# Output products of a stage's second token half, ranked behind the transpositions of the first half's next norm

## The chip, the cores and the metric

The kernel runs on one core of a Trainium2 chip. The metric is the device time of one execution in microseconds (us), lower is better; the time of a kernel is the median over its runs.

## The reference

A chain of ten residual stages over S = 256 tokens of width D = 1024, in fp32: FFN, differential attention, FFN, FFN, spatial gating (SGU), FFN, HGRN2, convolutional FFN, NSA (sparse attention), convolutional FFN. Each stage normalizes the stream, modulates it, runs its mixer, and adds the gated output back:

```
mod = silu(c) @ ada_w[i] + ada_b[i]
sh1, sc1, g1, sh2, sc2, g2, sh3, sc3, g3 = jnp.split(mod, N_MOD, axis=-1)
h = modulate(rms_norm(x, ln_ffn1[i]), sh1, sc1)
x = x + 0.5 * g1[:, None, :] * swiglu(h, ffn1_wg[i], ffn1_wu[i], ffn1_wd[i])
h = modulate(rms_norm(x, ln_mix[i]), sh2, sc2)
...
x = x + g2[:, None, :] * mix
h = modulate(rms_norm(x, ln_ffn2[i]), sh3, sc3)
x = x + 0.5 * g3[:, None, :] * swiglu(h, ffn2_wg[i], ffn2_wu[i], ffn2_wd[i])
x = rms_norm(x, ln_out[i])
```

Here `modulate(h, shift, scale)` is `h * (1 + scale) + shift` and `swiglu` is `(silu(h @ wg) * (h @ wu)) @ wd` with D_FF = 2816. Every stage ends in such an output matrix (`wd`, `w_o`, `w_out`), and the next stage can begin only with a norm over whole rows of the x that this matrix completes.

## The kernel before

**Tokens and products.** The 256 tokens are two halves of 128, h = 0 and h = 1 (first and second half). Each fp32 factor is split in a high and a low part (`whi`, `wlo` of a weight, `hhi`, `hlo` of the normed input, `ahi`, `alo` of the inner activation), and each product is three matmuls: high by high, high by low, low by high. The high part of a weight is made by ScalarE (ACT), the low part, `wlo<-raw,whi`, by VectorE (DVE). Weights come in 1 MB loads (`raw`).

**The end of a stage.** The output matrix accumulates in four PSUM tiles `pd`, two column blocks for each half. `down` adds inner blocks for both halves as they come, and keeps back the last few (`SKEW`: 4, 5 or 6). For the kept blocks it first finishes the first half (`down_rest(0)`); the second half's products of these blocks are `rest`: two column blocks of SKEW x 3 matmuls with 512 columns, 24, 30 or 36 in all. The closure `end` in `run` then writes, for each half: `residual` (`gy<-pd,gb`, the gate, and `x<-x,gy`, the sum, on DVE, twice 512 columns), and `norm`. Between the first half's residual and its norm it calls `rest()`.

**The norm.** `x_rstd` squares x on ACT with a row sum (`xs<-x`, then a read of the accumulator), `rstd` adds the two sums on DVE (`ss<-ss`) and takes the power -1/2 on GpSimd (POOL `ss<-ss,mhalf`). `norm` scales x into `xs` (first 512 columns on DVE, second on ACT), transposes it by eight matmuls of 128 columns (`xT<-ident,xs`), modulates each transposed block on ACT (`h<-xT,mcol`, eight of them), casts pairs on DVE (`hhi<-h`) and subtracts (`hlo<-h,hhi`, two of them). After stages 2 and 5 `norm_twice` does two norms in one, with the product `xrow<-x,raw` before. The next stage's first products take `hhi` of the first half. They are called `pqk` and `pv` (attention), `pgv` (FFN, SGU), `pig` (HGRN2) and `px` (conv FFN and NSA); a boundary is written 0→1 for the end of stage 0 and the start of stage 1.

**Who sets the order.** Nothing is issued as written. The class `Plan` records all operations with a rank, by which a list scheduler then puts each engine's program in one fixed order (`order`): an engine that comes free in the planner's own clock takes the operation of lowest rank whose inputs are there and whose tiles have slots.

```
op.prio = len(self.ops) + self.shift
```

`shift` is 0 but where a few places raise it (`NSA`, `FIRST`), so the rank is otherwise the number of the operation as written. Slots of tiles are handed out by rank too. All operations are issued by one helper, so the profile shows line 514 for each; tile names tell them apart. The last stage (i = 9) ends in the output and has no norm behind it in this form; stage 8 calls `end` with the halves swapped and a `rest` of its own, 48 products that also wait for two reloaded weights.

Of the kernel before, what the change touches and what calls it, by code (L numbers as in the profile page):

```python
# [525 lines left out]
ADA_PE = (9,)  # L526
RATE = 0.92
FIRST = 20

SKEW = {0: 4, 1: 4, 2: 6, 3: 4, 4: 4, 5: 6, 6: 4, 7: 5, 9: 4}  # L530
NSA = (250, 150, 20)
# [2 lines left out]
class Model:  # L534
# [458 lines left out]
    def first(self, wg, wu):  # L993
# [80 lines left out]
        def products(k):  # L1074
            nc.shift = FIRST
            for h in range(2):
                hs = slice(128 * h, 128 * h + 128)
                for c in range(3):
                    o = acc[h][c]
                    hi, lo = parts[k][c]  # L1080
                    nc.tensor.matmul(o, hhi[:, k, hs], hi, start=k == 0, stop=False)
                    nc.tensor.matmul(o, hhi[:, k, hs], lo, start=False, stop=False)
                    nc.tensor.matmul(o, hlo[:, k, hs], hi, start=False, stop=k == 7)
            nc.shift = 0
# [765 lines left out]
    def run(self, out):  # L1850
        nc, a = self.nc, self.a
        self.x = [self.C.tile([128, D], F32, name=f"x{h}") for h in range(2)]
        self.setup()
        self.warm(4)
        self.load_c()
        self.warm(10)
        blocks = {0: 29, 1: 16, 2: 33, 3: 33, 4: 12, 5: 33, 6: 20, 7: 33, 8: 15, 9: 33}
        prep = {4: self.sgu_prep, 6: self.hgrn_prep, 8: self.nsa_prep}
        self.acc, self.mcols, self.bcol, self.grow, self.col = {}, [], {}, {}, {}
        self.halves = (0, 1)  # L1860
        acts = self.first(a["ffn1_wg"][0], a["ffn1_wu"][0])
        for i in range(10):
            self.bg = []
            self.now = i
            if i in self.grow:
                self.bg.append(lambda i=i: self.gate_load(i))
            for item in ADA[i]:
                self.bg += self.mod_steps(item, item[1] in ADA_PE)
                if item == ("g", i):
                    self.bg.append(lambda i=i: self.gate_load(i))  # L1870
            if i == 0:
                self.bg[5:5] = [lambda: self.load_columns(("ln_mix", "ln_ffn2"), "cols1", [a["ada_b"][1]], 3)]
                self.bg[12:12] = [self.load_columns2]
                self.bg[15:15] = [self.attn_bias]
                self.bg[18:18] = [self.attn_lambda]
            if i == 2:
                self.bg[4:4] = [
                    lambda: self.load_columns(("norm_mix_2", "norm_ffn_2"), "cols3", [a["ada_b_2"][0]], 6),
                    lambda: self.load_columns(("sgu_ln_g", "hg_lb_2"), "cols4", [a["ada_b_2"][1]], 8)]
            self.bg_rate = len(self.bg) / (blocks[i] * RATE)  # L1880
            self.bg_due = 0.0
            if i in prep:
                prep[i]()
            row = None
            if i in (2, 5):
                row = self.load_row(a["ln_out"][i // 3])
            if i == 9:
                row = self.load_row(a["final_norm_2"])

            def end(halves=(0, 1), rest=self.down_rest, i=i, row=row):  # L1890
                self.flush()
                gb_now = self.gb
                if i < 9:
                    self.norm_begin()
                self.halves = halves
                for h in halves:
                    self.residual(h, gb_now)
                    if h == halves[0]:
                        rest()
                    if i == 9:  # L1900
                        y = self.xs()
                        r = self.x_rstd(h, y)
                        for c in range(2):
                            cs = slice(512 * c, 512 * c + 512)
                            nc.vector.scalar_tensor_tensor(y[:, cs], self.x[h][:, cs], r, row[:, cs], op0=OP.mult,
                                                           op1=OP.mult)
                            nc.sync.dma_start(out[0, 128 * h:128 * h + 128, cs], y[:, cs])
                    elif i in (2, 5):
                        self.norm_twice(h, row)
                    else:  # L1910
                        self.norm(h)

            if i in (0, 2, 3, 5):
                l, j = divmod(i, 3)
                nm = "ffn1" if j == 0 else "ffn2"
                self.ffn(a[nm + "_wg"][l], a[nm + "_wu"][l], a[nm + "_wd"][l], end, acts if i == 0 else ())
            elif i == 1:
                self.attention(end)
            elif i == 4:
                self.sgu(end)  # L1920
            elif i == 6:
                self.hgrn(end)
            elif i == 8:
                self.nsa(end)
            else:
                l = (i - 7) // 2
                self.conv_ffn(l, a["ffn_w_up_2"][l], a["ffn_w_down_2"][l], end)
# [24 lines left out]
```

## Time and profile before

| | |
|---|---|
| time, median of 3 runs | 1709.83 us (1709.03 to 1711.03) |
| time of the profiled execution | 1712.62 us |
| its span in the trace | 1710.8 us |
| TensorE (PE) busy | 1678.8 us, 98% |
| weight loads of TensorE (PEld) | 1508.2 us, 88% |
| VectorE (DVE) | 1309.8 us, 77% |
| ScalarE (ACT) | 947.0 us, 55% |
| GpSimd (POOL) | 65.1 us, 4% |
| mean granted clock of TensorE | 0.992 of 2.4 GHz |

The span is what the trace shows of one execution; 1.8 us of that execution's time lie outside it. A row of a timeline gives the start, the duration, the engine, the operation (output <- inputs, sizes), how many in a row, and in brackets how long the engine was idle before it and for what. Matmuls overlap one another in the pipe: one of 512 columns takes 0.39 us, but the next one starts 0.23 us after it.

### The profile page before, as it was taken

The numbers are of one execution on the slowest core, as the hardware profiler recorded it, in microseconds if no ns is written. First come the engines' busy times: TensorE is split into PE (matmuls) and PEld (weight loads), VectorE is DVE, ScalarE is ACT, GpSimd is POOL, SyncE is SP. The second block draws the span as 40 slices with busy tenths as digits, with TensorE's granted clock in tenths as the row PEclk, the third lists the DMA queues.
The fourth block names the chain that finished last, engine by engine and source line by source line (L and its number), as shares of the span: only waits on it lengthen the run. The fifth ranks groups of instructions, "written<-read, shape, count | busy, mean of one in ns | idle before, by whom it ended". The sixth has DMA issues, their size and how long they took to land.

```text
span 1710.8 us, 30956 instructions
## 1 busy us (share of the span) xinstructions
PE 1678.8 (98%) x12662; PEld 1508.2 (88%) x12662; DVE 1309.8 (77%) x1951; ACT 947.0 (55%) x1581; POOL 65.1 (4%) x60
## 2 busy tenths in 40 slices
PE   8999999999999999999999999999999999999998
PEld 6899789899988999788999889989998886689986
DVE  4887689987777877677877787889897547888754
ACT  4544467564445544374644368877554556766542
POOL 0000012100001000001000000000000000000000
PEclk9999999999999999999999999999999998999999
DMA  9998865678896998676688975357888565257662
GB/s 319 332 323 297 274 229 201 209 245 264 295 327 203 340 305 315 220 243 223 225 281 307 317 240 174 110 181 247 275 287 314 176 202 218 87 168 227 221 210 74
DMA packets 258191, 415.25 MB, mean 243 GB/s; under 512 B 12938, under 2 KB 204277, under 8 KB 257025
## 3 DMA queue, kind: packets, MB, share of 16 engines
q1 hardware_dynamic: 258049, 413.27, 71.7%
q8 instruction: 99, 1.62, 0.4%
q14 instruction: 43, 0.35, 0.1%
HBM read 412.14 MB, written 1.10 MB: 242 GB/s over the span
## 4 chain that ended last, share of the span: by engine, by line
PE 67%; DVE 4%; DMA 4%; ACT 3%; issue 1%; POOL 0%; DVEq 0%; POOLq 0%; ACTq 0%; SPq 0%
PE pd L514 18%; PE pv L514 16%; PE pg L514 8%; PE pa L514 7%; PE pq L514 3%; PE pig L514 3%; DMA raw<-in_ffn_wd 2%; DVE wlo L514 2%; PE pf L514 1%; DMA raw<-in_ffn_wu 1%; PE pgv L514 1%; ACT whi L514 1%; DMA raw<-in_ada_w 1%; PE px L514 1%; PE no L514 1%
## 5 line engine op out<-in xcount | busy, mean ns | idle before, releaser
L514 ACT ACTIVATE whi<-raw 128x1024 fp32r<-128x1024 f32 x508 | 530.8, 1057 | 525.8 <-PE pd L514 136.9
L514 DVE TENSOR_TENSOR wlo<-raw,whi 128x1024 fp32r<-128x1024 f32 x508 | 611.8, 1220 | 216.6 <-ACT whi L514 212.2
L514 DVE SCALAR_TENSOR_TENSOR acc<-raw,csil,acc 128x1024 f32<-128x1024 f32 x192 | 246.0, 1281 | 16.1 <-DMA raw<-in_ada_w 13.5
L514 PE MATMUL pv<-hhi,wlo 128*128 128x256 f32 x896 | 252.6, 282 | 0.0
L514 PE MATMUL pv<-hlo,whi 128*128 128x256 f32 x896 | 252.2, 281 | 0.0
L514 PE MATMUL pv<-hhi,whi 128*128 128x256 f32 x896 | 252.1, 281 | 0.0
L514 PE MATMUL pd<-whi,ahi 128*128 128x512 f32 x604 | 239.5, 398 | 0.7 <-ACT whi L514 0.7
L514 PE MATMUL pd<-wlo,ahi 128*128 128x512 f32 x604 | 238.2, 394 | 0.1
L514 PE MATMUL pd<-whi,alo 128*128 128x512 f32 x604 | 237.9, 395 | 0.0
L514 PE MATMUL pg<-hhi,whi 128*128 128x256 f32 x608 | 172.2, 283 | 0.0
L514 PE MATMUL pg<-hhi,wlo 128*128 128x256 f32 x608 | 171.8, 283 | 0.0
L514 PEld LDWEIGHTS pv<-hhi,whi 128*128 128x128 f32 x896 | 170.4, 190 | 1.2 <-issue 1.2
L514 PE MATMUL pg<-hlo,whi 128*128 128x256 f32 x608 | 171.5, 282 | 0.0
L514 PEld LDWEIGHTS pv<-hhi,wlo 128*128 128x128 f32 x896 | 170.4, 190 | 0.0
L514 PEld LDWEIGHTS pv<-hlo,whi 128*128 128x128 f32 x896 | 170.3, 190 | 0.0
L514 PEld LDWEIGHTS pd<-whi,ahi 128*128 128x128 f32 x604 | 113.4, 188 | 32.9 <-issue 6.1
L514 PEld LDWEIGHTS pd<-whi,alo 128*128 128x128 f32 x604 | 113.4, 188 | 25.9 <-issue 0.2
L514 PEld LDWEIGHTS pd<-wlo,ahi 128*128 128x128 f32 x604 | 113.4, 188 | 25.4 <-DVE wlo L514 0.5
L514 PEld LDWEIGHTS pg<-hhi,whi 128*128 128x128 f32 x608 | 115.6, 190 | 2.6 <-issue 1.7
L514 PEld LDWEIGHTS pg<-hhi,wlo 128*128 128x128 f32 x608 | 115.6, 190 | 0.1
L514 PEld LDWEIGHTS pg<-hlo,whi 128*128 128x128 f32 x608 | 115.6, 190 | 0.0
L514 PE MATMUL pa<-hhi,whi 128*128 128x256 f32 x352 | 99.3, 282 | 0.0
(361 smaller groups left out, 3126.1 us busy)
## 6 DMA issues: line engine op xcount, KB each, us to landing
raw<-in_ada_w SPq DMA_DIRECT2D x118, 1024.0 KB
raw<-in_ffn_wd SPq DMA_DIRECT2D x44, 1024.0 KB
raw<-in_ffn_w_up SPq DMA_DIRECT2D x44, 1024.0 KB
raw<-in_ffn_wg SPq DMA_DIRECT2D x41, 1024.0 KB
raw<-in_ffn_wu SPq DMA_DIRECT2D x41, 1024.0 KB
raw<-in_ffn_w_down SPq DMA_DIRECT2D x22, 1024.0 KB
raw<-in_hg_w_in SPq DMA_DIRECT2D x16, 1024.0 KB
raw<-in_attn_w_qkv SPq DMA_DIRECT2D x12, 1024.0 KB
```

What stands on the lines that cost most here:

```text
L514: f(*[real(v) for v in args], **{k: real(v) for k, v in kw.items()})
```

## The change

One constant and two assignments: while `rest()` is recorded, 80 is added to the rank of each of its operations. The norm of one half is about 28 operations, so the second half's kept products stand behind the first half's norm in rank, about beside the second half's norm, which needs them, and the first operations of the next stage. Nothing is added to or taken from the computation.

```diff
 ADA_PE = (9,)
 RATE = 0.92
 FIRST = 20
+REST = 80
 
 SKEW = {0: 4, 1: 4, 2: 6, 3: 4, 4: 4, 5: 6, 6: 4, 7: 5, 9: 4}
 NSA = (250, 150, 20)
@@ -1896,7 +1897,10 @@
                 for h in halves:
                     self.residual(h, gb_now)
                     if h == halves[0]:
+
+                        nc.shift = REST
                         rest()
+                        nc.shift = 0
                     if i == 9:
```

The planner turns these ranks into orders. TensorE at 0→1: the last rows of `rest` (`pd`) and the first half's transpositions.

```order
 L514 MATMUL pd<-whi,alo 128x512
 L514 MATMUL pd<-whi,ahi 128x512
-L514 MATMUL pd<-wlo,ahi 128x512
-L514 MATMUL pd<-whi,alo 128x512
-L514 MATMUL pd<-whi,ahi 128x512
-L514 MATMUL pd<-wlo,ahi 128x512
-L514 MATMUL pd<-whi,alo 128x512
 L514 MATMUL xT<-ident,xs 128x128 x8
+L514 MATMUL pd<-wlo,ahi 128x512
+L514 MATMUL pd<-whi,alo 128x512
+L514 MATMUL pd<-whi,ahi 128x512
+L514 MATMUL pd<-wlo,ahi 128x512
```

The eight transpositions moved ahead of the last five products of `rest`; a fifth follows the four that are shown. At the other boundaries the tail behind the transpositions is 8 products (2→3), 10 (3→4), 5 (4→5), 9 (5→6), 12 (7→8) and about 33 (8→9). At 6→7 and in stage 9's end nothing moved.

TensorE at 1→2, before: the last product of the first half (`pd_3434` is its second column block), then `rest` (`pd_3450` and `pd_3556`, 24 products), then the transpositions.

```order
L514 MATMUL pd_3434<-wlo_3665,ahi_3713 128x512
L514 MATMUL pd_3434<-whi_3629,alo_3724 128x512
L514 MATMUL pd_3450<-whi_3529,ahi_3458 128x512
L514 MATMUL pd_3450<-wlo_3616,ahi_3458 128x512
...
L514 MATMUL pd_3556<-wlo_3665,ahi_3713 128x512
L514 MATMUL pd_3556<-whi_3629,alo_3724 128x512
L514 MATMUL xT_3790<-ident_84,xs_3748 128x128 x2
```

After, at the same place; the second half's blocks are `pd_3525` (four rows here) and `pd_3532` (seven rows).

```order
L514 MATMUL pd_3434<-wlo_3672,ahi_3728 128x512
L514 MATMUL pd_3434<-whi_3619,alo_3740 128x512
L514 MATMUL pd_3525<-whi_3573,alo_3740 128x512
L514 MATMUL pd_3525<-whi_3619,ahi_3728 128x512
...
L514 MATMUL pd_3532<-wlo_3672,ahi_3728 128x512
L514 MATMUL pd_3532<-whi_3619,alo_3740 128x512
L514 MATMUL xT_3801<-ident_84,xs_3777 128x128 x2
```

Between the first half's last product and its transpositions there were 24 products of `rest`, and now there are 11; the other 13 run earlier, before or among the first half's. After these transpositions eight products of the next stage are issued before the second half's transpositions; before the change there were 33.

VectorE at 2→3, before: the second half's residual (`gy`, `x1`, `xrow`) among the first half's casts (`hhi`, `hlo`).

```order
L514 TENSOR_TENSOR wlo_5797<-raw_5626,whi_5781 128x1024
L514 TENSOR_TENSOR gy_5815<-pd_5350,gb_4536 128x512
L514 CAST hhi_5818<-h32_5811 128x2x128
L514 TENSOR_TENSOR x1_103<-x1_103,gy_5815 128x512
L514 CAST hhi_5818<-h32_5811 128x2x128
L514 TENSOR_TENSOR hlo_5836<-h32_5811,hhi_5818 128x4x128
L514 CAST hhi_5818<-h32_5822 128x2x128 x2
L514 TENSOR_TENSOR hlo_5836<-h32_5822,hhi_5818 128x4x128
L514 TENSOR_TENSOR xrow_5861<-x1_103,raw_3537 128x512
L514 TENSOR_SCALAR ss2_5793<-ss2_5793 128x1
L514 TENSOR_TENSOR wlo_5871<-raw_5626,whi_5854 128x1024
```

After, at the same place:

```order
L514 CAST hhi_5807<-h32_5797 128x2x128
L514 TENSOR_TENSOR wlo_5811<-raw_5626,whi_5781 128x1024
L514 CAST hhi_5807<-h32_5797 128x2x128
L514 CAST hhi_5807<-h32_5814 128x2x128
L514 TENSOR_TENSOR hlo_5831<-h32_5797,hhi_5807 128x4x128
L514 CAST hhi_5807<-h32_5814 128x2x128
L514 TENSOR_TENSOR hlo_5831<-h32_5814,hhi_5807 128x4x128
L514 TENSOR_TENSOR gy_5855<-pd_5350,gb_4536 128x512
L514 TENSOR_TENSOR lbt_5863<-cols4_4408 128x8
L514 TENSOR_TENSOR x1_103<-x1_103,gy_5855 128x512
L514 TENSOR_TENSOR xrow_5874<-x1_103,raw_3543 128x512
L514 TENSOR_TENSOR wlo_5877<-raw_5626,whi_5852 128x1024
```

The second half's last `gy` and `x1` moved behind all of the first half's casts, `xrow` behind them, and the low part of the next weight (`wlo_5871`, now `wlo_5877`) behind `xrow`. On ACT the squares of the second half, one or two of which stood ahead of the first half's eight `h`, now all stand behind them. The order at 5→6 moved in the same way; at 0→1 and 4→5 `gy` and `x1` moved behind two or three of the casts. The queue of loads (SP) did not change but for one exchange of two rows, and POOL's changed in one row.

## Rows read from the trace of the kernel before

**Rows 1.** The page, busy times: engine, us, share of the span, instructions.
```profile
PE 1678.8 (98%) x12662; PEld 1508.2 (88%) x12662; DVE 1309.8 (77%) x1951; ACT 947.0 (55%) x1581; POOL 65.1 (4%) x60
```

**Rows 2.** Waits of TensorE: tile that waited, releaser, us in total, times, longest.
```profile
PE xT L514 <- DVE xs L514: 3.7, 4, 1.3
PE pgv L514 <- DVE hhi L514: 2.5, 4, 0.9
...
PE px L514 <- DVE hhi L514: 1.8, 2, 1.0
...
PE pqk L514 <- DVE hhi L514: 1.3, 1, 1.3
...
PE pig L514 <- DVE hhi L514: 1.0, 2, 0.6
```

**Rows 3.** Timeline of TensorE, then of ACT, at 0→1.
```profile
226.89 1.04 PE L514 MATMUL xT<-ident,xs 128*128 128x128 f32 x8
229.25 0.39 PE L514 MATMUL pqk<-whi,hhi 128*128 128x256 f32 x1 [1.32 <-DVE hhi L514]
...
227.87 2.88 ACT L514 ACTIVATE h<-xT,mcol 128x128 f32<-128x128 f32 x8
```

**Rows 4.** Timeline of TensorE at 1→2.
```profile
338.89 0.39 PE L514 MATMUL pd<-whi,alo 128*128 128x512 f32 x1
...
344.67 1.03 PE L514 MATMUL xT<-ident,xs 128*128 128x128 f32 x8
346.27 0.38 PE L514 MATMUL pgv<-whi,hhi 128*128 128x256 f32 x1 [0.57 <-DVE hhi L514]
...
351.36 1.09 PE L514 MATMUL xT<-ident,xs 128*128 128x128 f32 x8 [0.87 <-DVE xs L514]
```

**Rows 5.** Timelines of ACT and of POOL at 1→2.
```profile
343.77 0.70 ACT L514 ACTIVATE xs<-x,ss 128x512 f32<-128x512 f32 x1
...
342.54 0.56 POOL L514 TENSOR_TENSOR ss<-ss,mhalf 128x1 f32<-128x1 f32 x1 [8.75 <-DVE ss L514]
349.32 1.47 POOL L514 TENSOR_TENSOR ss<-ss,mhalf 128x1 f32<-128x1 f32 x1 [6.22 <-DVE ss L514]
```

**Rows 6.** Timeline of TensorE at 2→3.
```profile
538.68 0.39 PE L514 MATMUL pd<-whi,alo 128*128 128x512 f32 x1
538.91 1.03 PE L514 MATMUL xT<-ident,xs 128*128 128x128 f32 x8
540.54 0.38 PE L514 MATMUL pgv<-whi,hhi 128*128 128x256 f32 x1 [0.59 <-DVE hhi L514]
...
545.23 0.39 PE L514 MATMUL pgv<-wlo,hhi 128*128 128x256 f32 x1 [0.55 <-DVE wlo L514]
...
547.00 0.61 PE L514 MATMUL xT<-ident,xs 128*128 128x128 f32 x4
...
548.61 0.38 PE L514 MATMUL pgv<-whi,hhi 128*128 128x256 f32 x1 [0.45 <-DVE hhi L514]
```

**Rows 7.** Timelines of DVE and of ACT at 2→3.
```profile
542.62 0.69 DVE L514 TENSOR_TENSOR hlo<-h,hhi 128x512 fp32r<-128x512 f32 x1
543.23 0.68 DVE L514 TENSOR_TENSOR xrow<-x,raw 128x512 f32<-128x512 f32 x1
...
537.04 1.07 ACT L514 ACTIVATE whi<-raw 128x1024 fp32r<-128x1024 f32 x1 [0.87 <-PE pd L514]
```

**Rows 8.** Timelines of TensorE and of DVE at 4→5.
```profile
816.27 0.38 PE L514 MATMUL pgv<-whi,hhi 128*128 128x256 f32 x1 [0.92 <-DVE hhi L514]
821.69 1.09 PE L514 MATMUL xT<-ident,xs 128*128 128x128 f32 x8 [0.66 <-ACT xs L514]
...
819.26 1.21 DVE L514 TENSOR_TENSOR wlo<-raw,whi 128x1024 fp32r<-128x1024 f32 x1
```

**Rows 9.** Two windows in stage 8: busy us (instructions) by engine, granted clock, DMA.
```profile
1428.00:1432.00 4.00, 2.42 (x28) 1.93 (x24) 2.00 (x5) 2.71 (x6) 0.00 (x0) 1.00 0.86 343
1432.00:1448.00 16.00, 15.95 (x67) 7.71 (x67) 10.60 (x38) 9.52 (x27) 0.00 (x0) 0.57 0.67 244
```

## The prediction

> **What bounds the kernel now.** I read the busy times first: TensorE works for 98% of the span [rows 1], so time can only be won where it stands still, or lost where it comes to stand still. Next I read what it waits for [rows 2]. The waits that this change can touch are of two kinds. One is the wait of the next stage's first product for the cast `hhi`: 2.5 us for `pgv`, 1.8 for `px`, 1.3 for `pqk`, 5.6 in all. The other is the wait of the transpositions for `xs`, 3.7 us in four places.
>
> The timeline shows how the first kind comes about. At 0→1 the transpositions start at 226.89 and the first product of attention at 229.25 [rows 3]: TensorE has issued everything of the old stage and can only wait for ACT's `h`, 2.88 us for eight, and the first cast. The same gap is 1.60 us from transposition to product at 1→2 [rows 4] and 1.63 at 2→3 [rows 6], of which the eight transpositions themselves take 0.87 (eight starts 0.109 apart, an estimate from the block of 1.04 us, whose last piece runs out in the pipe [rows 3]).
>
> The second kind follows some 7 us later. The last product of `rest` at 2→3 starts at 538.68, and the second half's transpositions at 547.00, 8.3 us later [rows 6]. All of that is the second half's chain: gate, sum, squares, power, scaling. TensorE fills it with the first half's 48 products of the next stage, but runs dry or short just there: 0.55 us idle for `wlo` at 545.23, then 0.45 behind the transpositions [rows 6], 0.87 at 1→2 [rows 4], 0.66 at 4→5 [rows 8]. So the two halves' chains are both nearly on the path. Whoever fills the first gap with `rest` starts the second chain later.
>
> **The change part by part.** It adds and removes no instruction, so all that counts is the order. Prices: a 512-column product of `rest` is 0.23 us (226.89 in [rows 3] is the slot after such products; 338.89 to 344.67 in [rows 4] is 25 and a bit of them, 5.78 us), a 256-column one about 0.12, an estimate at half the columns.
>
> *The tail in the gap.* At 0→1 five products, 1.15 us, now lie behind the transpositions, in a wait of 1.32 [rows 3]. The first product of attention comes that much earlier. The last product of `rest` comes 0.87 later, the eight transpositions that now go ahead. I take a gain of 0.3 us here, since 49 products of the next stage now cover the chain where 38 did.
>
> *2→3, laid end to end.* Eight tail products. The transpositions start 1.83 us earlier, at 537.08, but ACT is still in `whi` from 537.04 to 538.11 [rows 7], so `h` starts at 538.1 and not at 537.5. The first cast is then possible at 538.9, and the tail ends at 539.8; the first `pgv` starts there, 0.7 us before the old 540.54 [rows 6]. Now DVE: in the new order the cast is followed by `wlo` (1.22), casts, `hlo` (0.69), cast, `hlo`, and these follow ACT's `h` (0.36 each from [rows 3]) to 542.1. Then come `gy`, `x1` and `xrow` at about 0.68 each: 542.8, 543.5, 544.1. Before, `xrow` ended at 543.91 [rows 7], and the square of the first 512 columns of x, which ACT could do early, ran beside it. Now it starts only behind `x1`, the square of `xrow` behind that, and both `ss` behind `wlo`, which itself has moved behind `xrow` and ends near 545.3. The second half's transpositions come out at 548.5 and not 547.00, and the first second-half product 1.61 later [rows 6], at 550.1 instead of 548.61. The 34th product still waits for `wlo` at 545.2. So the 0.7 us is lost again and 1.5 us with it: **+1.5**. Bounds: if the chain kept its length, 0.87 later less the 0.7 gained, +0.2; with the second power also late, +2.5.
>
> *5→6* has the same orders, a tail of nine and the same stage end: **+1.3**, with the same bounds.
>
> Here a rule is weighed. The power on POOL took 0.56 us at 342.54 and 1.47 at 349.32 [rows 5], the second time beside a DVE operation with two SBUF inputs. In the new order at 2→3 nothing of that kind stands beside it, so 0.9 us could come back there and at 5→6, and the sum below would be 1.8 lower. The Trainium skill (SBUF — State Buffer, "Who interferes with whom") says that DVE and GpSimd share one pair of ports under an exclusive lock; the two durations agree with it. I do not take the 1.8, since both sums and both powers now stand in a row behind the last square, where one power was out of the way before.
>
> *4→5.* Tail five, gap 0.92 [rows 8]. The first product comes about 0.65 earlier. `x1` moves behind two casts and both `hlo`, some 2 us later than before, the next `wlo` stays near 819 [rows 8], and `ss` falls behind it. The second half's transpositions come at about 823.0 and not 821.69 [rows 8]. By then all 48 first-half products are done; before, 13 stood behind the transpositions as cover. First second-half product: 823.0 + 1.6 = 824.6, against 821.69 + 0.87 + 13 x 0.12 = 824.1. **+0.6** (0 to +1.5).
>
> *1→2.* This is the other way round: no tail, but 13 products of `rest` moved ahead, out of the place between the first half's last product and its transpositions. That last product started at 338.89 [rows 4], and `xs` was complete at 343.77 + 0.70 = 344.47 [rows 5]: a chain of 5.58 us. It was covered by 24 products; eleven products and the last one cover 12 x 0.23 = 2.75. A wait of 2.8 us opens, or 2.1 if the `whi` that ACT did just ahead of `xs` goes elsewhere; I take 2.6. Then comes the old gap of 0.7. Eight products of the next stage, 1 us, stand before the second half's transpositions, which by the old 6.9 us (344.44 to 351.36 [rows 4], the slot before 344.67) are due 1.5 us later still. Together 4.8, against the old gap of 0.7 and the 0.87 idle before the second transpositions [rows 4], 1.6: **+3.2**. Below, +1, if the second chain runs free; above, +4.5.
>
> *The others.* 3→4 and 8→9 have tails of 10 and 33; no rows here price them, and I set +0.5 and +0.4, between 0→1 and 2→3. 6→7 is unchanged, 7→8 even. Inside stages 1 and 8 the order moved too, without a term I could name: 0, with ±1.5 each.
>
> *Sum.* -0.3 + 3.2 + 1.5 + 0.5 + 0.6 + 1.3 + 0 + 0 + 0.4 = **+7.2 us**. The profiled execution took 1712.62, so 1719.8 of its kind; it lies 2.8 above the median of the runs. On the median, 1709.83 + 7.2 = **1717.0**.
>
> **The rivals.** *A, the gaps just close (faster).* The tails fill the waits for `hhi`, and the second chain, started 0.87 us later but freed from waiting behind other work, is no longer than it was. Then the 5.6 us of [rows 2] go but for 6→7, about 5 in all: 1704.8. For it: the gaps are real, and a tail of five to twelve products fits into them. Against it: the second half's waits of 0.45 to 0.87 [rows 4, 6, 8], which say that this chain has no slack. It decides where `gy` and `x1` of the second half come on DVE: ahead of the first half's `hlo`, A holds; behind, not.
>
> *B, given back to the digit (no change).* The wait moves from the first cast to the second transpositions at the same size, and 1→2 finds its waits filled by the 13 moved products' old places: 1710. For it: at 0→1 and 7→8 my own terms nearly cancel.
>
> *C, the clock (slower still).* In stage 8 four microseconds with TensorE busy for 2.42 were followed by 16 at a granted clock of 0.57, that is mostly at 1.2 GHz of 2.4 [rows 9]; 16 x 0.43 = 6.9 us went. At 1→2 the new order has three waits, 4.8 us, within some nine. If the clock falls there too, 1717.0 + 6.9 = 1723.9. The Trainium skill (TensorE: Matmul & The Clock Gate, "HAM oscillation") has a kernel whose idle stretches between bursts drop the clock in this way; in this trace it stays at full level through all of the gaps of the boundaries, which are shorter.
>
> **How the numbers follow.** My forecast has 0.47, A 0.17, B 0.22, C 0.14. A measurement here can tell about 0.2%, 3.4 us, from no change. Forecast and C are slower, 0.61; B the same, 0.22; A faster, 0.17. The forecast's own range, by its bounds, is 1711.5 to 1721. For 8 in 10 it goes down to 1707.5, which takes in B and leaves most of A out, and up to 1722.5, which leaves half of C out.
>
> **What the profile would show.** Right: first products earlier by 0.6 to 1.2 us after the transpositions' own start at 0→1, 2→3, 4→5; the waits for `hhi` below 2 us in the list; the waits of `xT` for `xs` up from 3.7 to 9 or more; a wait of 2 to 3 us ahead of the first half's `xT` at 1→2; second transpositions at 2→3 some 9.8 us after the old place of `rest`'s last product. Wrong: waits of `xT` no higher than before, or 1→2 without a wait, which would be A; or a stretch at half clock behind 1→2, which is C. What I trust least is DVE's order read as time: if `wlo` comes earlier than its place suggests, 2→3 and 5→6 shrink to nothing and B is near.

## The result and the profile after

The changed kernel took 1718.67 us (median of 6 runs, 1717.25 to 1722.04), the kernel before 1709.74 beside it (6 runs, 1708.72 to 1712.77): ratio 1.0051, 95% interval 1.0041 to 1.0062, so 7 to 10.6 us slower, 8.9 by the medians. Forecast were 1717.0 and a range of 1707.5 to 1722.5.

The page of the changed kernel, busy times, answers to [rows 1]; the work is the same.

```profile
PE 1679.1 (98%) x12662; PEld 1510.1 (88%) x12662; DVE 1309.0 (76%) x1951; ACT 947.7 (55%) x1581; POOL 64.2 (4%) x60
```

Its waits of TensorE answer to [rows 2]:

```profile
PE xT L514 <- DVE xs L514: 6.0, 3, 3.8
PE pgv L514 <- DVE hhi L514: 3.2, 4, 1.1
...
PE xT L514 <- ACT xs L514: 2.0, 4, 0.5
PE pgv L514 <- DVE wlo L514: 1.9, 2, 1.6
...
PE pig L514 <- DVE wlo L514: 1.5, 1, 1.5
```

The wait for attention's first cast, 1.3 us before, is gone. The transpositions wait 6.0 us for DVE's half of `xs` instead of 3.7, 3.8 of them at one place, and 2.0 instead of 0.7 for ACT's half. Two waits for `wlo` have grown from 0.6 and 0.5 to about 1.5 each.

To see where the time went, I cut both traces at the first half's transpositions of each boundary; the start of their first one is the mark. The marks of before that were not shown yet (TensorE's timeline; 4→5, 5→6, 6→7, 7→8, 8→9):

```profile
814.31 1.03 PE L514 MATMUL xT<-ident,xs 128*128 128x128 f32 x8
...
1011.62 1.04 PE L514 MATMUL xT<-ident,xs 128*128 128x128 f32 x8
...
1159.63 1.06 PE L514 MATMUL xT<-ident,xs 128*128 128x128 f32 x8 [1.27 <-DVE xs L514]
...
1353.22 1.03 PE L514 MATMUL xT<-ident,xs 128*128 128x128 f32 x8
...
1511.90 1.03 PE L514 MATMUL xT<-ident,xs 128*128 128x128 f32 x8
```

The same marks of the changed kernel, from 0→1 on (3→4 left out):

```profile
223.46 1.03 PE L514 MATMUL xT<-ident,xs 128*128 128x128 f32 x8
...
347.15 1.49 PE L514 MATMUL xT<-ident,xs 128*128 128x128 f32 x8 [3.79 <-DVE xs L514]
349.71 0.58 PE L514 MATMUL pgv<-whi,hhi 128*128 128x256 f32 x1 [1.07 <-DVE hhi L514]
...
541.44 1.03 PE L514 MATMUL xT<-ident,xs 128*128 128x128 f32 x8
...
818.80 1.03 PE L514 MATMUL xT<-ident,xs 128*128 128x128 f32 x8
...
1016.30 1.04 PE L514 MATMUL xT<-ident,xs 128*128 128x128 f32 x8
...
1166.77 1.06 PE L514 MATMUL xT<-ident,xs 128*128 128x128 f32 x8 [1.27 <-DVE xs L514]
...
1357.92 1.03 PE L514 MATMUL xT<-ident,xs 128*128 128x128 f32 x8
...
1509.36 0.66 PE L514 MATMUL xT<-ident,xs 128*128 128x128 f32 x4 [0.51 <-ACT xs L514]
```

After the change a mark comes earlier by the tail that lies behind it. So each stretch is corrected by its products at 0.2285 us, about the distance of their starts (from 0→1 to 1→2, for example, five more: 347.15 - 223.46 - 1.15 = 122.5).

| stretch between marks | before, us | after, corrected, us | difference |
|---|---|---|---|
| start to 0→1 | 226.9 | 224.6 | -2.3 |
| 0→1 to 1→2 | 117.8 | 122.5 | +4.8 |
| 1→2 to 2→3 | 194.2 | 196.1 | +1.9 |
| 2→3 to 4→5 | 275.4 | 276.7 | +1.3 |
| 4→5 to 5→6 | 197.3 | 198.4 | +1.1 |
| 5→6 to 7→8 | 341.6 | 342.3 | +0.7 |
| 7→8 to 8→9 | 158.7 | 156.2 | -2.4 |
| 8→9 to the end | 198.9 | 199.2 | +0.3 |

They sum to +5.4, but for rounding the 5.3 by which the two spans differ (1710.8 and 1716.1). The two gains are mostly the granted clock of the traced executions. Up to 0→1 TensorE's program is the same in both kernels; here are the windows 32 to 40 us of before, then of after, where 8 x 0.21 = 1.7 us lie:

```profile
32.00:40.00 8.00, 7.89 (x51) 5.52 (x52) 3.27 (x6) 2.27 (x5) 0.00 (x0) 0.79 1.07 356
```

```profile
32.00:40.00 8.00, 8.00 (x64) 5.85 (x62) 3.51 (x8) 3.52 (x7) 0.00 (x0) 1.00 1.07 359
```

In stage 8 the half-clock stretch of before [rows 9] is shorter in this execution, 16 us at 0.79 from 1434 on, 3.4 us less. Without these two the spans would differ by 5.3 + 1.7 + 3.4 = 10.4, an estimate; the medians differ by 8.9.

The loss stands in two neighbouring stretches, from 0→1 to 2→3: +6.7 us. Two of the smaller rows show no loss of the order. From 2→3 to 4→5 the changed kernel has a half-clock stretch:

```profile
744.00:752.00 8.00, 8.00 (x56) 7.75 (x55) 5.24 (x8) 5.62 (x11) 0.55 (x1) 0.79 0.54 172
```

Two kernels below with the same order of TensorE there, but without such a stretch (the rank raised everywhere but at stage 0; the change with ten at stage 0), take 1.5 and 1.7 us less from mark to mark, and so 0.3 and 0.4 less than before. From 4→5 to 5→6 three kernels with the change's order took 194.9 to 195.2 us from mark to mark, not corrected, and the change 197.5; the five with the order of before, itself among them, took 196.1 to 198.1. So +1.1 lies within what executions of one order differ by.

Around 1→2, the changed kernel's timelines of TensorE, ACT and DVE:

```profile
342.96 0.40 PE L514 MATMUL pd<-whi,alo 128*128 128x512 f32 x1
...
341.99 1.06 ACT L514 ACTIVATE whi<-raw 128x1024 fp32r<-128x1024 f32 x1 [3.80 <-PE pd L514]
342.96 0.61 ACT L514 ACTIVATE xs<-x 128x512 f32<-128x512 f32 x1
...
343.57 1.04 ACT L514 ACTIVATE whi<-raw 128x1024 fp32r<-128x1024 f32 x1
344.51 0.61 ACT L514 ACTIVATE xs<-x 128x512 f32<-128x512 f32 x1
...
341.97 0.69 DVE L514 TENSOR_TENSOR x<-x,gy 128x512 f32<-128x512 f32 x1
...
345.25 0.21 DVE L514 TENSOR_SCALAR ss<-ss 128x1 f32<-128x1 f32 x1 [0.66 <-ACT xs L514]
```

TensorE issues its last product at 342.96 and stands until 347.15. The first half's x is complete at 341.97 + 0.69 = 342.66, but its second square starts only at 344.51. In ACT's order one `whi` stands ahead of the first square and another between the two, and the first of them had waited 3.80 us for TensorE to give back a slot. No run moved these `whi` alone, so what they cost is read from the timeline and not tested.

The granted clock in windows of 4 us there:

```profile
344.00:348.00 4.00, 0.85 (x6) 0.88 (x7) 2.89 (x5) 4.00 (x10) 0.93 (x1) 0.95 0.00 0
348.00:352.00 4.00, 2.93 (x14) 2.53 (x13) 3.90 (x10) 3.39 (x10) 1.49 (x1) 0.50 0.66 192
352.00:356.00 4.00, 4.00 (x27) 4.00 (x26) 2.79 (x5) 2.20 (x7) 0.00 (x0) 0.69 0.50 151
```

TensorE worked 0.85 us of the first four. Then it ran at 1.2 GHz in all of the next four (0.50) and in part of the four after (0.69).

### The profile page after: what moved, and what is told of

The parts are those of the page before. It is cut to its first block, busy times and chain, and to the rows that moved or that the text cites. A ratio compares the mean times of both kernels' runs of the same rounds, so it can differ in the third digit from the quotient of the medians.

```text
span 1716.1 us, 30936 instructions
## 1 busy us (share of the span) xinstructions
PE 1679.1 (98%) x12662; PEld 1510.1 (88%) x12662; DVE 1309.0 (76%) x1951; ACT 947.7 (55%) x1581; POOL 64.2 (4%) x60
## 4 chain that ended last, share of the span: by engine, by line
PE 80%; DMA 8%; DVE 7%; ACT 3%; issue 1%; POOL 1%; SPq 1%; DVEq 0%; POOLq 0%; ACTq 0%
PE pd L514 22%; PE pv L514 18%; PE pg L514 9%; PE pa L514 7%; PE pgv L514 3%; DVE wlo L514 3%; PE pq L514 3%; PE pig L514 3%; DMA raw<-in_ffn_wg 2%; DMA raw<-in_ada_w 2%; PE pqk L514 2%; ACT whi L514 1%; PE pf L514 1%; DVE acc L514 1%; DMA raw<-in_ffn_wd 1%
```

## The experiments

All are compared with the kernel before in the same measurement. Executions of one kernel spread over some 10 us in these measurements (1705 to 1716 for before), so the intervals carry the verdicts, and the traces the places.

Within one kernel the slower executions mostly have the lower mean granted clock. The 83 executions of before in these measurements lie between 0.992 and 0.997, the six of the change between 0.989 and 0.993. So part of the loss of a slower kernel can be half-clock stretches. Only one execution of each kernel was traced; where it was one of the fastest, that is said below.

**The rank raised at stage 0 alone.**

```diff
-                        nc.shift = REST
+                        nc.shift = REST if i == 0 else 0
```

> The rank is raised at the end of stage 0 alone, five tail products behind the transpositions at 0→1; nothing is raised at 1→2, yet the plan of the attention moves too and leaves 11 products and then 8 around the transpositions at 1→2, as in the change. Theory (most of the loss is this knock-on, 3.8 us of wait and a clock drop at 1→2): +5 to +7 us against before, a wait for xs of 3 us or more at 1→2. Rival (each boundary pays for its own late second half, as the prediction summed): 0→1 alone is worth -0.3, and with 1→2's term +3, so about +3 and no clock drop. Rival (0→1 alone only gains): -0.5.

Ratio 1.0068, interval 1.0049 to 1.0086: +8.4 to +14.7 us, as slow as the whole change. At 1→2, where this kernel raises nothing, TensorE's timeline has the same wait:

```profile
349.01 1.92 PE L514 MATMUL xT<-ident,xs 128*128 128x128 f32 x8 [3.79 <-DVE xs L514]
351.58 0.58 PE L514 MATMUL pgv<-whi,hhi 128*128 128x256 f32 x1 [0.64 <-DVE hhi L514]
```

The assignment at one boundary is paid for at the next, since the planner's order of all of the attention moved: from 0→1 to 1→2 this kernel's TensorE has the order of the change. The same two stretches carry the loss in its trace, +6.3 and +1.6 us with the correction of the table; about 1.5 of the 6.3 go with a half-clock stretch inside the attention (284 to 292 us, at 0.79) that the trace of the change does not have. The loss was more than I had expected, and more than the wait alone explains.

**The rank raised everywhere but at stage 0.**

```diff
+                        nc.shift = 0 if i == 0 else REST
```

> The rank is raised everywhere but at the end of stage 0, so that the attention's plan stays as before up to its end; at 1→2 two products stand behind the transpositions and 47 products before the second half's. Theory (knock-on of 0→1 is most of the loss): +1 to +3 us, with the half-clock stretch gone from 1→2. Rival (late second halves are most of it): +7 to +9, as the change.

1.0017, interval 1.0002 to 1.0032: +0.3 to +5.5 us. The theory holds, and the trace, of the second fastest execution of ten, has no half-clock stretch at 1→2; the later boundaries cost a little, 2.9 us at the middle of the interval.

**The second half's residual ranked earlier.**

```diff
                 for h in halves:
+                    if h != halves[0]:
+                        nc.shift = -22
                     self.residual(h, gb_now)
+                    nc.shift = 0
```

> The change, with the second half's residual ranked 22 operations earlier, ahead of the first half's casts; tails of 5 to 13 products stay behind the first transpositions, 33 or 34 products stand before the second half's, and 1→2 is as before. Theory (the gain in the first gap is real and is lost by the second half's gate and sum standing behind the casts): faster than before by 2 to 5 us, 1705 to 1708. Rival (the second half is late because its products are, whatever DVE does): within 2 us of before or slower.

1.0033, interval 1.0017 to 1.0049: slower, and the expectation failed. The trace shows a gain and a loss. At 4→5 the second half's transpositions no longer wait, and the first product comes as early as in the change:

```profile
817.59 0.39 PE L514 MATMUL pgv<-whi,hhi 128*128 128x256 f32 x1 [0.32 <-DVE hhi L514]
...
821.99 1.28 PE L514 MATMUL xT<-ident,xs 128*128 128x128 f32 x8
```

0.32 us idle stand against 0.92 + 0.66 in [rows 8]. But 1→2 has a wait of 3.55 us, since only 8 products of cover stood there in the new order, which I had not counted when I wrote that it was as before:

```profile
347.13 1.94 PE L514 MATMUL xT<-ident,xs 128*128 128x128 f32 x8 [3.55 <-DVE xs L514]
```

They do not explain the median of 1715.07. The traced execution is the fastest of eight, 1710.47 us at a granted clock of 0.994; the others go up to 1719.47 at 0.988. So here most of the loss goes with the clock, in executions that were not traced, and its places are not shown.

**The rank raised at stages 2 and 5 alone.**

```diff
+                        nc.shift = REST if i in (2, 5) else 0
```

> The rank is raised at the ends of stages 2 and 5 alone (the double norm). Prediction's terms: +1.5 and +1.3, +2.8 in all. From the trace of the change (+0.5 and +1.1): +1.6. Rival (the closed first gap wins): -1.4. 3→4 and 6→7 not touched by name; a shift of more than 3 us either way would mean the plan's knock-on is large here too.

1.0031, interval 1.0014 to 1.0048: +2.4 to +8.2 us. The sign is the prediction's, and the lower end is near its +2.8; the +1.6 that I took from the trace of the change lies outside. The traced execution is the fastest of ten (1710.21 us at a granted clock of 0.995; the two slowest, 1719.98 and 1722.75, had 0.990 and 0.989), so the place of what goes beyond the two boundaries stays open.

**Ten instead of eighty at stage 0 alone.**

```diff
+                        nc.shift = 10 if i == 0 else 0
```

> The rank is raised at the end of stage 0 alone, by 10 instead of 80: four tail products behind the transpositions at 0→1 instead of five, and the attention keeps its 24 products of cover before the transpositions at 1→2. Theory (the loss is the attention's plan that the tail of five sets off, not the tail): within 1 us of before, with the first gap at 0→1 closed to 0.4 us and no wait over 1.1 us at 1→2. Rival (a tail behind the transpositions at 0→1 is what costs): +7 to +11, as with the rank raised by 80 there.

1.0003, interval 0.9993 to 1.0012: -1.2 to +2.1 us. The four tail products stand behind the first two of the eight transpositions, not behind all of them, and the loss is gone. 1→2 looks as before, to compare with [rows 4]:

```profile
344.70 1.04 PE L514 MATMUL xT<-ident,xs 128*128 128x128 f32 x8
346.31 0.39 PE L514 MATMUL pgv<-whi,hhi 128*128 128x256 f32 x1 [0.57 <-DVE hhi L514]
...
351.39 1.09 PE L514 MATMUL xT<-ident,xs 128*128 128x128 f32 x8 [0.87 <-DVE xs L514]
```

A tail of five is 1.15 us of work, and eight or more were lost with it. So it is not the tail behind the transpositions that costs, but the order of the attention that the planner made after it: the change and the kernel with stage 0 alone share one order of TensorE from 0→1 to 1→2, and this kernel has another.

**The rank raised at stage 1 alone.**

```diff
+                        nc.shift = REST if i == 1 else 0
```

> The rank is raised by 80 at the end of stage 1 alone: two tail products and 22 of cover at 1→2, 47 products of the next stage before the second half's transpositions. The prediction's term for 1→2 as due to this assignment: +3.2. Theory (1→2 loses only when the attention's plan was set off before it): -0.5 to +1, no wait over 1.1 us before either transposition.

1.0001, interval 0.9989 to 1.0013: -1.9 to +2.2 us. The assignment at 1→2 itself does nothing to the time that can be told here, and the +3.2 is out.

**Stages 4 and 5 alone, with the earlier residual.**

```diff
+                        nc.shift = -22 if i in (4, 5) else 0        (before the residual)
+                        nc.shift = REST if i in (4, 5) else 0
```

> Rank raised by 80 and the second half's residual ranked 22 earlier, at the ends of stages 4 and 5 alone: tails of 5 and 13, 33 products before the second half's transpositions. Theory (the first gap is worth winning where the second half's gate and sum don't fall behind the casts; the stages' lengths in the trace of e3 were 2.1 and 1.3 us below before): -3.3 us, 1705 to 1706.5. Rival (what one boundary gains the next gives back): within 1 us of before.

0.9994, interval 0.998 to 1.0008: between -3.4 and +1.4 us. It does not tell the two apart; -3.3 is at the very edge.

**The wait at 1→2 filled.**

```diff
+            if op.method == "transpose" and op.args[0].tl.kw["name"] == "xT":
+                seen += 1
+                if seen == 33:
+                    for _ in range(30):
+                        self.nc.tensor.transpose(real(op.args[0]), real(op.args[2]), real(op.args[2]))
```

> The change with 30 idle transpositions of the identity put on TensorE into the wait at 1→2, 3.3 us of the 3.8, nothing else moved; they write what the real transpositions overwrite. Theory (part of the loss at 1→2 is the half clock behind the wait, 347 to 354 us): the granted clock stays at full there and 1.5 to 3 us come back against the change, +6 to +7.5 against before; the wait itself stays. Rival (the clock costs nothing, since TensorE waits there anyway): as the change, +9.

1.0051, interval 1.0036 to 1.0066: the same as the change. The interval, +6.1 to +11.3 us, does not by itself exclude the theory's +6 to +7.5; the trace speaks against it. The filled kernel's timeline, and behind it its window of 16 us:

```profile
344.30 0.40 PE L520 MATMUL pd<-whi,alo 128*128 128x512 f32 x1
344.54 3.44 PE L517 MATMUL xT<-ident 128*128 128x128 f32 x30
348.40 1.09 PE L520 MATMUL xT<-ident,xs 128*128 128x128 f32 x8 [0.43 <-DVE xs L520]
351.06 0.39 PE L520 MATMUL pgv<-whi,hhi 128*128 128x256 f32 x1 [1.56 <-DVE hhi L520]
```

```profile
340.00:356.00 16.00, 13.49 (x82) 11.89 (x81) 13.56 (x24) 10.35 (x24) 2.42 (x2) 0.90 0.40 133
```

The granted clock in that window rose to 0.90 (the same window of the changed kernel has 0.79), but it fell behind the next two waits, and the first product came 351.06 - 344.30 = 6.76 us after the last product of `rest`, against 349.71 - 342.96 = 6.75 in the change. ACT and DVE set that; the slow transpositions lay in waits. From 1→2 to 2→3 the two kernels have one order of TensorE and take the same time, 194.4 and 194.3 us. This tests the clock at this one place and not elsewhere.

**Cover taken away by hand.** The kernel before, planned as it was; only in TensorE's finished order 12 of the 24 products that stand between the first half's last product and its transpositions at 1→2 are put ahead of the last `oT`.

```diff
+        rest = pe[at - 24:at]
+        last = rest[-1].args[1].tl, rest[-2].args[1].tl
+        ahead = [op for op in rest if op.args[1].tl not in last]
+        k = max(k for k in range(at) if w(pe[k]) == "oT")
...
+        out[k:k] = ahead
```

> The kernel before with one hand move and no new plan: at 1→2, on TensorE alone, 12 of the 24 products of the second half that stand between the first half's last product and its transpositions are put ahead of the last head pair's transposition (oT), nothing else moves. Theory (this lost cover is what the change pays at 1→2): the first half's transpositions wait 2.7 to 3.5 us, and the time is +2.5 to +4. Rival (the products fill waits elsewhere, the cover is worth nothing): within 1 us of before.

1.0009, interval 0.9997 to 1.0021: -0.5 to +3.6 us. The trace has the wait, smaller than expected, 1.67 us, and behind it one that is longer than before:

```profile
347.22 1.06 PE L530 MATMUL xT<-ident,xs 128*128 128x128 f32 x8 [1.67 <-DVE xs L530]
349.67 0.39 PE L530 MATMUL pgv<-whi,hhi 128*128 128x256 f32 x1 [1.38 <-DVE hhi L530]
```

1.67 + 1.38 against 0.57 in [rows 4], +2.5. The cover is worth that much in the trace; the timing alone can't tell it from nothing. Lost cover by itself, 3.6 us at most, is therefore less than half of what stage 0's assignment costs, 8.4 at least.

**The change with ten at stage 0.**

```diff
+                        nc.shift = 10 if i == 0 else REST
```

> The change with the rank raised by 10 instead of 80 at the end of stage 0 alone, by 80 at all the others: four tail products at 0→1, 22 of cover at 1→2, all later boundaries as in the change. Theory (the change without its knock-on in the attention): +1 to +2.5. Rival (the later boundaries are what costs): +6 or more.

1.0017, interval 1.0004 to 1.003: +0.7 to +5.1 us. The later boundaries together cost a few us, 2.9 at the middle of the interval; the rest of the change's 8.9, some 6 us by the middles of two wide intervals, is the knock-on in the attention. Stage 0 alone cost 8.4 or more, so the costs of single assignments do not simply add up.

**What won, put together.**

```diff
+                        nc.shift = -22 if i in (3, 4, 7) else 0     (before the residual)
+                        nc.shift = {0: 10, 3: REST, 4: REST, 7: REST}.get(i, 0)
```

> What won in the traces put together: rank raised by 10 at stage 0; by 80, with the second half's residual ranked 22 earlier, at stages 3, 4 and 7; the others as before. From the waits at the boundaries of e3 and e5: -0.3 at 0→1, -0.5 at 3→4, -1.7 at 4→5, -0.3 at 7→8, together -2.8, 0.16%. Rival (the plan gives it back elsewhere, as in e7): within 1 us of before.

0.9999, interval 0.9989 to 1.0008, -1.9 to +1.4 us: no gain, the rival is right. In its trace the window 740 to 748 us, behind 3→4, has TensorE busy throughout at a granted clock of 0.79, which costs 1.7 us there:

```profile
740.00:748.00 8.00, 8.00 (x55) 7.75 (x54) 5.69 (x8) 5.84 (x11) 0.55 (x1) 0.79 0.46 146
```

**Ten at every stage.**

```diff
-REST = 80
+REST = 10
```

> The change with 10 in place of 80 at every stage: tails of four products at 0→1, 3→4, 4→5, 7→8 and 8→9, none at 2→3 and 5→6, 22 of cover at 1→2. Theory (tails that fit the first gap win up to 0.9 us where the second half keeps its cover): -1 to -3. Rival (first gap's gain goes to the second half): within 1 us of before.

1.003, interval 1.0016 to 1.0043: slower, the opposite of what I expected. In its trace 186.6 us pass from the first output product of stage 8 to that of stage 9, 184.2 before; why the plan of stage 8 got longer stays open. The traced execution is the third fastest of twelve (1711.46 us at a granted clock of 0.995); the four slowest, 1717.30 to 1719.60, had 0.990 to 0.992, so part of the loss goes with the clock.

## Why the prediction was right, step by step

**The direction and the size are right, the bookkeeping only in part.** +7.2 was forecast, +8.9 measured. That the sum came so near is partly luck: the terms up to 2→3 add up to +2.9 where the trace has +6.7, and the later ones to +4.3 where the table has +3.4 without stage 8, 2.4 of it in the two rows that show no loss of the order.

*1→2, the largest term.* The wait that opens was put at 2.6 us and the gap behind it at 0.7; they are 3.79 and 1.07. The 1.5 us before the second half's transpositions did not come. In sum 4.86 against 4.8. The prediction gave the upper end of the first as 2.8, with the chain of 5.58 as before; what made it longer are the two `whi` in ACT's order, ahead of the squares and between them (341.99 to 344.51); before, the one `whi` there came behind both, ahead of the scaling.

But the term stands in the wrong account. It was worked out from the order of this kernel, where it does stand; as a statement on what raising the rank at stage 1 does, it is refuted: that alone gives 1.0001. The cause is the assignment at stage 0, which I had costed at -0.3. The attention's own order, "0, with ±1.5", was not 0: stage 0's assignment alone costs +8.4 or more, and 10 in place of 80 there takes it away. That this assignment costs the time is shown; how much of it is the wait at 1→2 and how much the clock in executions that were not traced stays open.

*0→1.* The first gap closed as forecast, 1.32 us of wait to none, and the second half's transpositions wait 0.48 where they hardly waited before. Alone, in the kernel with four tail products, that is not to be told from nothing.

*2→3 and 5→6, +1.5 and +1.3: too much.* The changed kernel's timelines of TensorE, DVE and POOL at 2→3, and behind them the POOL row of before:

```profile
549.80 0.38 PE L514 MATMUL pgv<-wlo,hhi 128*128 128x256 f32 x1 [1.59 <-DVE wlo L514]
551.70 1.09 PE L514 MATMUL xT<-ident,xs 128*128 128x128 f32 x8
553.43 0.38 PE L514 MATMUL pgv<-whi,hhi 128*128 128x256 f32 x1 [0.64 <-DVE hhi L514]
...
547.92 0.69 DVE L514 TENSOR_TENSOR xrow<-x,raw 128x512 f32<-128x512 f32 x1
548.53 1.22 DVE L514 TENSOR_TENSOR wlo<-raw,whi 128x1024 fp32r<-128x1024 f32 x1
...
550.02 1.11 POOL L514 TENSOR_TENSOR ss<-ss,mhalf 128x1 f32<-128x1 f32 x2 [10.29 <-DVE ss L514]
...
544.18 1.96 POOL L514 TENSOR_TENSOR ss<-ss,mhalf 128x1 f32<-128x1 f32 x2 [8.77 <-DVE ss L514]
```

The first second-half product comes 553.43 - (541.44 + 1.83) = 10.16 us after the mark's place with the tail counted, against 548.61 - 538.91 = 9.70 in [rows 6]: +0.46, not +1.5. DVE's order did what was said: `xrow` and `wlo` came late, and TensorE stands 1.59 us for that `wlo`. The error is in the powers: two of them took 1.11 us together, with no large DVE operation of two SBUF inputs beside them, and 1.96 before, when `wlo<-raw,whi` ran beside them (543.96 to 545.18). At 5→6 they took 1.10, and 2.02 before. So the 0.9 us per boundary that I weighed and set aside was there, and 1.5 - 0.9 = 0.6 and 1.3 - 0.9 = 0.4 would have been the terms; from 5→6 to 6→7 the marks give 1166.77 - 1016.30 - 2.06 = 148.4 against 148.0, +0.4. The Trainium skill (SBUF — State Buffer, "Who interferes with whom") says that DVE and GpSimd share one pair of ports under an exclusive lock; these durations agree with it.

Alone, the two assignments cost +2.4 to +8.2, more than these rows. The order at 2→3 is another one there, and in that trace the stretch from 2→3 to 3→4 is 1.3 us longer than before.

*4→5, +0.6.* The transpositions of the second half come 828.35 - 818.80 - 1.15 = 8.4 us after the mark's old place, against 7.4 before ([rows 8] and the marks), 1.0 later; 1.3 was forecast. The first gap shrank to 0.33 us. Whether time was lost by it is not shown, as said under the table.

*The signs.* The waits of `pgv` for `hhi` did not fall below 2 us but rose to 3.2, and those of `xT` for DVE's `xs` rose to 6.0 and not to 9. The second transpositions at 2→3 came 551.70 - (541.44 + 1.83 - 0.23) = 8.7 us after the old place of `rest`'s last product, and not 9.8. The wait at 1→2 came, longer than 2 to 3 us, and with it the half clock, which I had named as a sign of C.

*The rivals.* A, the gaps just close, is true of the first gaps and false of the time: even with the cause of the loss removed (ten at stage 0, or the earlier residual at some stages) nothing faster could be measured. B holds for the change without its knock-on, nearly. C was half right: the clock fell at 1→2 as that rival said. The Trainium skill (TensorE: Matmul & The Clock Gate, "HAM oscillation") has a kernel in which it falls behind idle stretches; here it fell behind the wait of 3.79 us. Yet with the wait filled, about half of the lost clock came back and no time did. At 0.79 over 16 us no more than 3.4 us can have gone there; 6.9 was far too much for this place.

## What to carry to other kernels

With a planner that orders everything, a rank raised at one place is a new plan for all that follows: cost the order that comes out, place by place, and do not credit a term to the line that was edited until that line has run alone. Here a rank of 10 instead of 80 at one stage, four tail products instead of five, was the difference between 1.0003 and 1.0068. A wait that is filled in front can be paid at the next chain that shares the same engines; look at what stands ahead of the squares or sums on the engine with a fixed order, since there a wait for a slot holds up work that needs none.

Single executions of one instruction order can differ by several us through the granted clock, so two traces are compared stretch by stretch before any difference of spans is read. Look also at which execution was traced: where it is the fastest of its kernel, its trace can't show what makes the median slow.

## What was not expected of the hardware

The half-clock stretch in stage 8, which cost 6.9 us in the trace of before [rows 9], does not have its length from the order. In the kernel with the rank raised at stage 1 alone, whose order in stage 8 is that of before, the same windows read:

```profile
1428.00:1432.00 4.00, 4.00 (x58) 3.78 (x55) 2.81 (x5) 1.53 (x3) 0.00 (x0) 1.00 0.39 113
1432.00:1448.00 16.00, 14.37 (x81) 7.87 (x81) 12.39 (x42) 12.53 (x33) 0.00 (x0) 0.79 0.75 301
```

16 x 0.21 = 3.4 us, half of it.

Behind 3→4 the clock fell, in the changed kernel and in the one that put the winners together, in part of a window in which TensorE was busy throughout (8.00 of 8 us). What it did before the fall, in the changed kernel:

```profile
744.42 2.05 PE L514 MATMUL Rp<-raw 2*128 2x128 f32 x16
```

These are sixteen products with two rows each, which count as busy like any other. In six traces they stand in one block like this. Behind it the clock fell in three (the change, the filled kernel, the winners put together), and the stretch from 3→4 to 4→5 took 81.1 us; in the other three it did not, and the stretch took 79.5 to 79.6. In the eight traces where they stand in two or three pieces it never fell there. That the block is the cause is not shown by this.
